# A decoder block on one core: x of the second half scaled sooner, the conv debt's floor lowered, two gate row buffers, and products of the identity in the opening

## The chip, the cores and the metric

One core of one Trainium2 chip runs the whole block. The metric is the device time of one execution in microseconds (us), lower is better. PE is TensorE (matmul), DVE is VectorE, ACT is ScalarE, POOL is GpSimd, SP is the queue engine that issues most transfers.

## The reference

The sequence has 2048 rows of 1024 channels, all in float32. Cut to what matters here:

```python
mod = silu(c) @ w_ada + b_ada
shift, scale, gate = split(mod, 3)
h = rms_norm(x, norm_w) * (1 + scale) + shift
a, b, g_conv, q, k, v, g_attn, m_conv, m_attn = split(h @ w_in)
u = depthwise_causal_conv(a * sigmoid(b), conv_w, conv_b)      # 31 taps
u = silu(layer_norm(u)) * silu(g_conv);  y_conv = u @ w_conv_out
q, k = rope(rms_norm(q), positions), rope(rms_norm(k), positions)
o = softmax-merge of 3 dilated window attentions (12 heads)
y_attn = (o * silu(g_attn)) @ w_attn_out
y = sigmoid(m_conv) * y_conv + sigmoid(m_attn) * y_attn
out = x + gate * (y @ w_out)
```

## The kernel before

All products keep float32 accuracy by splitting each operand into a high and a low part and adding three products (high by high, high by low, low by high). One block of 512 columns thus costs 12 matmuls, all issued from one line (L345); the kernel calls such a block a slot. Most of the projection is a Strassen-like scheme: a quad of blocks in seven products instead of eight, with sums of x and of the weights made by DVE and POOL.

The projection runs as 566 slots in four stages: q, k and v of the first half of the sequence (slots 0 to 131), its conv inputs and gates (132 to 285), then q, k, v (286 to 411) and conv and gates (412 to 565) of the second half. A planner written in Python walks over the slots. At each slot it prepares weights three slots ahead, runs what an agenda holds for that slot (`at_slot`), and spends a credit of VectorE time on two lists of spare work: the conv taps (`ce`, `cq`, `co`) and the "later" operations, which are the scaling and Strassen sums of the second half's x (tiles `xl`, `xs`, 32 operations). The credit grows by `PACE` of the stage (and by `AFTER` in quiet slots), falls by the cost of what was issued, and has a floor and a ceiling.

PE always executes in program order. The other engines do so in slots 0 to 137 and 286 to 417; in the two gate stretches between, a list scheduler with its own estimates chooses their order.

**The opening.** Before slot 0, x's first 512 columns are squared (ACT), summed on PE (`x_sum`, L1017), copied by DVE as a row (`xrow`, L1022), transposed back by PE (L1026), made an inverse root (`xst`, L1028 and POOL), and spread over the partitions by PE (`x_spread`, L1034); DVE then multiplies x by it (L1039). Meanwhile PE multiplies the conditioning vector by its matrix (`ada_mm`, L1045), ACT copies the row (L1050), PE transposes it (`pt_ada`, L1056) and DVE makes `mod` (L1059, L1061). Quarters A11, A12, A21 and A22 of h are split by ACT (`A_hi`) and DVE (`A_lo`) in `first_part` (A11 and A12 at L1077 to L1082, A21 and A22 at L1084 and L1085; A12 and A22 need the second group of `mod`). The same chain runs for t=1, the second 512 columns, during slots 0 to 3 (its scaling is L1041). Between these, DVE reduces the rotary angles in steps of two 1024-wide operations and more (`angle_steps`, L1109 to L1113), with a sine on ACT (L1111); ACT then reorders the tables (`table_turn`, L1121, L1123).

**Around slot 53.** DVE applies the rotary tables, makes low parts of weights and x sums (`slB`, `S_lo`), and prepares the inverse root of k (`rwk`, L210 as all helper-issued DVE work), which PE spreads into `rsk` at L737.

**The gate row.** From slot 444 on DVE adds 16 rows of w_ada, 128x512 each, into `gate_sum`, each through a tile `wg` that a transfer fills (`gate_load` L1587, `gate_add`). The tag `wg` has one buffer.

Of the kernel before, what the change touches and what calls it, by code (L numbers as in the profile page):

```python
# [40 lines left out]
FIRST_GATES, BETWEEN = (1, 1), ((1, 2, 1, 2, 1, 2, 1, 3), (1, 1, 2, 1, 1, 2, 1, 4))  # L41
PACE, AFTER, AGAIN = (2.87, 3.15, 2.62, 2.85), (0.75, 0.1), 12
PLAIN_QK, LATER_END = 4, 65
# [20 lines left out]
def tile_hybrid_block(  # L64
# [444 lines left out]
    def at_slot(s, f, where="vec"):  # L509
        agenda.setdefault((s, where), []).append(f)  # L510
# [620 lines left out]
    def angle_steps(count):  # L1131
        for _ in range(count):
            f = next(turning, None)
            if f:
                f()
# [142 lines left out]
    for name in ("B21", "B22"):  # L1278
        for j in range(2):
            weight(j, name)  # L1280

    angle_steps(7)
    pm = bank("t", "xm0")
# [5 lines left out]
    for k in range(2):  # L1289
        ada_mm(0, acc, k)  # L1290
    st = x_roots(0, pm, rows)
    angle_steps(2)
    for k in range(2, 4):
        ada_mm(0, acc, k)
    pr = x_spread(0, st, bank("u", "xr0"))
    for k in range(4, KC):
# [3 lines left out]
    for k in range(4):  # L1300
        x_scale(k, 0, pr)
    ada_mod(0, ada_row(0, acc), "t")
    for k in range(4):
        first_part("A11", k, 0)
# [51 lines left out]
    for k in range(4, KC):  # L1356
        at_slot(1, lambda k=k: x_scale(k, 0, pr), "act")
    for s, count in ((0, 2), (1, 2), (2, 6)):
        at_slot(s, lambda count=count: angle_steps(count))
# [123 lines left out]
    def run_later(s):  # L1483
        k, f = later_todo.pop(0)
        f()
        if k < 2 and later_todo[0][0] != k:
            at_slot(s + 3, lambda: later_load(k + 2), "store")
            later_from[k + 2] = s + 6

# [94 lines left out]
    def gate_load(i):  # L1584
        k, half = divmod(i, 2)
        wa = aside["wg", i] = aside["gp"].tile([P, 512], F32, tag="wg", name=f"wg{i}")
        nc.sync.dma_start(wa, w_ada[P * k : P * k + P, 2 * D + 512 * half : 2 * D + 512 * half + 512])  # L1587
# [10 lines left out]
    def gate_bias(i):  # L1598
        br = aside["gp"].tile([P, 512], F32, tag="wg", name=f"b_gate{i}")
        nc.sync.dma_start(br[:1, :], b_ada[None, 2 * D + 512 * i : 2 * D + 512 * i + 512])  # L1600
        dst = aside["g"][:1, 512 * i : 512 * i + 512]
        vec.tensor_add(dst, dst, br[:1, :])

    def gate_sum(i):
        sl = slice(512 * i, 512 * i + 512)
        pg = bank("o", f"pg{i}")
        nc.tensor.matmul(pg, ones, aside["g"][:, sl], start=True, stop=True)
        row = aside["gp"].tile([P, 512], F32, tag="wg", name=f"gate_out{i}")
        nc.scalar.activation(row[:1, :], pg[:1, :], AF.Copy, scale=0.125)
        nc.sync.dma_start(gate_d[:, sl], row[:1, :])  # L1610

    s = where_of[gates_start[1] + 6][6]
    at_slot(s, gate_open, "enter")
    for i in range(2 * KC + 1):
        if i:
            at_slot(s + 2 * i, lambda i=i: gate_add(i - 1))
        if i < 2 * KC:
            at_slot(s + 2 * i, lambda i=i: gate_load(i))
    for i in range(2):
# [9 lines left out]
    for s, (i, n) in enumerate(slots):  # L1629
# [15 lines left out]
        if n == 0:  # L1645
            kind, *job = jobs[i]
            running[i] = kind(*job, columns[i][0])
        next(running[i], None)
# [11 lines left out]
        stage = (i >= gates_start[0]) + (i >= half_jobs) + (i >= gates_start[1])  # L1660
        rest = AFTER[i >= half_jobs] if not waiting and s > busy_until[0] and stage % 2 else 0.0
        credit = min(max(credit, -2.0) + PACE[stage] + rest - spent[0], 2.0)
        spent[0] = 0.0
# [435 lines left out]
```

## Time and profile before

| | |
|---|---|
| time, median of 3 runs | 2354.8 us (2352.3 to 2357.51) |
| the profiled execution's own time | 2360.98 us |
| its span in the trace | 2358.4 us |
| mean granted TensorE clock | 0.993 of full |

The span is what the trace covers; 2.6 us of the execution's own time lie around it. The profiled execution was 6.2 us above the median of the runs shown. Times inside the trace are counted from the start of the span.

### The profile page before, as it was taken

What the parts mean: (1) busy time and instruction counts of PE and PEld (TensorE: products, weight loads), DVE (VectorE), ACT (ScalarE), POOL (GpSimd) and SP (SyncE); (2) the same over time, 40 slices, a digit from 0 to 9 for tenths busy, and PEclk for the clock granted to TensorE, in tenths of its full rate; (3) what the DMA queues carried; (4) which work ended last, traced back from release to release, by engine and by line L of the source; (5) the groups of instructions that cost most, each with busy time, mean ns of one, the idle gap of its engine ahead of it and who ended that gap; (6) DMA issues with size and microseconds to landing.
All of it is one profiled execution on the core that took longest, in us unless ns stands there. A gap on an engine that the chain in (4) does not pass through costs nothing.

```text
span 2358.4 us, 34462 instructions
## 1 busy us (share of the span) xinstructions
PE 2290.8 (97%) x11438; PEld 1868.6 (79%) x11438; DVE 1690.2 (72%) x2792; ACT 1120.8 (48%) x2291; POOL 1108.2 (47%) x866
## 2 busy tenths in 40 slices
PE   7999899999999999999999999999999999999999
PEld 4776688887878888787888887887888888888887
DVE  6668664566969789859746446799997957787544
ACT  5744455555644444654555545553444444332221
POOL 2345444545577789956433342445566630000221
PEclk9999999999999999999999999999999999999999
DMA  7567566665554455643666665655444579875553
GB/s 277 188 214 235 169 173 216 190 211 190 168 192 152 148 181 178 204 139 100 203 181 189 206 191 182 213 180 164 139 141 146 174 255 319 285 236 188 179 161 103
DMA packets 300942, 445.76 MB, mean 189 GB/s; under 512 B 28759, under 2 KB 132311, under 8 KB 300765
## 3 DMA queue, kind: packets, MB, share of 16 engines
q1 hardware_dynamic: 286648, 418.37, 55.8%
q10 hardware_dynamic: 14116, 25.20, 2.8%
q8 instruction: 90, 1.47, 0.3%
q14 instruction: 88, 0.71, 0.1%
HBM read 282.37 MB, written 161.09 MB: 188 GB/s over the span
## 4 chain that ended last, share of the span: by engine, by line
PE 50%; DVE 4%; DMA 2%; ACT 1%; issue 1%; POOL 0%; SPq 0%; ACTq 0%; DVEq 0%; POOLq 0%
PE yc L1710 8%; PE oa L1992 4%; PE ya L1710 4%; PE paab L345 3%; PE pak L345 3%; PE pav L345 3%; PE paq L345 2%; PE oc L1992 2%; PE pag_ma_d L345 2%; PE pcab L345 2%; PE pag_g_d L345 2%; PE po L945 2%; PE pcv L345 1%; DMA wg<-in_w_ada_dram 1%; PE pcq L345 1%; PE pck L345 1%
## 5 line engine op out<-in xcount | busy, mean ns | idle before, releaser
L282 POOL TENSOR_TENSOR slT<-wT,shT 128x512 fp32r<-128x512 f32 x172 | 232.8, 1354 | 283.9 <-ACT shT L281 270.6
L282 POOL TENSOR_TENSOR slB<-wB,shB 128x512 fp32r<-128x512 f32 x152 | 203.5, 1339 | 151.2 <-ACT shB L281 136.6
L281 ACT ACTIVATE shB<-wB 128x512 fp32r<-128x512 f32 x222 | 139.7, 630 | 167.5 <-issue 35.1
L282 POOL TENSOR_TENSOR slT<-wB,shT 128x512 fp32r<-128x512 f32 x98 | 131.8, 1350 | 148.1 <-ACT shT L281 120.6
L210 DVE SCALAR_TENSOR_TENSOR ce<-us,pair_taps,ce 128x512 f32<-128x512 f32 x240 | 180.9, 754 | 6.2
L210 DVE SCALAR_TENSOR_TENSOR ce<-ut,chan,ce 128x512 f32<-128x512 f32 x240 | 179.2, 747 | 0.5
L281 ACT ACTIVATE shT<-wT 128x512 fp32r<-128x512 f32 x176 | 110.4, 627 | 119.9 <-PE paab L345 21.2
L210 DVE SCALAR_TENSOR_TENSOR cq<-ut,chan,cq 128x512 f32<-128x512 f32 x208 | 155.2, 746 | 4.1 <-ACT cq L412 4.0
L210 DVE CUSTOM_DVE_ANT_0 sm<-ps,mask,rqq 128x256 f32<-128x256 f32 (+1 forms) x192 | 78.0, 443 | 93.0 <-PE ps L880 45.2
L276 POOL TENSOR_TENSOR wB<-wB,wB 128x512 f32<-128x512 f32 x80 | 111.2, 1391 | 47.2 <-DVE slB L210 44.1
L281 ACT ACTIVATE shT<-wB 128x512 fp32r<-128x512 f32 x120 | 75.2, 627 | 63.3 <-PE paab L345 30.7
L922 ACT ACTIVATE pT<-ptp 128x512 f32<-128x512 f32 (+2 forms) x84 | 44.8, 533 | 89.9 <-PE ptp L917 89.7
L139 POOL TENSOR_SCALAR stf<-stf 128x4 f32<-128x4 f32 x4 | 1.9, 473 | 179.9 <-DVE stf L1748 143.1
L945 PE MATMUL po<-v,pT 128*128 128x128 f32 x560 | 81.8, 277 | 3.0 <-ACT pT L922 2.8
L1920 ACT ACTIVATE yh<-yq 128x512 fp32r<-128x512 f32 x48 | 27.3, 623 | 120.4 <-POOL yq L1914 44.7
L945 PEld LDWEIGHTS po<-v,pT 128*128 128x128 f32 x560 | 75.1, 191 | 10.2 <-ACT pT L922 3.8
L210 DVE TENSOR_TENSOR slB<-wB,shB 128x512 fp32r<-128x512 f32 x70 | 54.9, 786 | 30.5 <-ACT shB L281 27.5
L902 ACT ACTIVATE sm<-sm,osb 128x256 f32<-128x256 f32 (+1 forms) x128 | 58.5, 463 | 4.2 <-DVE osb L210 4.2
L1911 POOL TENSOR_TENSOR ys<-yq 128x512 f32<-128x512 f32 x8 | 11.4, 1426 | 100.5 <-DMA yq<-y_d 88.8
L276 POOL TENSOR_TENSOR wT<-wB,wB 128x512 f32<-128x512 f32 x40 | 56.3, 1407 | 1.1
L917 PE MATMUL ptp<-ident,sm 128*128 128x128 f32 x332 | 52.3, 273 | 2.8 <-DVE stm L210 2.4
L622 POOL TENSOR_TENSOR slB_q<-wB_q,shB_q 128x512 fp32r<-128x512 f32 x16 | 29.5, 1846 | 54.3 <-ACT shB_q L621 49.7
(896 smaller groups left out, 7854.3 us busy)
## 6 DMA issues: line engine op xcount, KB each, us to landing
wB<-in_w_in_dram SPq DMA_DIRECT2D x262, 256.0 KB, 3.8
wT<-tT_d SPq DMA_DIRECT2D x136, 256.0 KB, 3.0
tT_d<-wB SPq DMA_DIRECT2D x102, 256.0 KB, 3.4
qk<-qk_d SPq DMA_DIRECT2D x96, 256.0 KB, 4.2
v_d<-vev SPq DMA_DIRECT2D x48, 256.0 KB, 3.4
qk_d<-spare_hi SPq DMA_DIRECT2D x48, 256.0 KB, 3.8
qk_d<-spare_lo SPq DMA_DIRECT2D x48, 256.0 KB, 4.1
v<-v_d SPq DMA_DIRECT2D x96, 128.0 KB, 3.9
```

Of the source, the lines that this page charges most:

```text
L210: return f(out, *args, **kw)
L276: nc.gpsimd.tensor_tensor(dst, x0, x1, op=ALU.subtract)
L281: nc.scalar.activation(h, q[name], AF.Copy)
L282: eng.tensor_tensor(l, q[name], h.bitcast(F32), op=ALU.subtract)
L345: nc.tensor.matmul(ps, x, y, start=(first and m == 0), stop=(last and m == 11), skip_group_check=True)
L622: nc.gpsimd.tensor_tensor(last[1], q[name], last[0].bitcast(F32), op=ALU.subtract)
L902: nc.scalar.activation(sm[:, a:z], sm[:, a:z], AF.Exp, scale=-1.0, bias=box["low"][i], accum_out=box["total"][i])
L917: nc.tensor.transpose(pt[:, c : c + P], box["sm"][:, c : c + P], ident)
L922: nc.scalar.activation(valid(pT), valid(pt), AF.Copy)
L945: nc.tensor.matmul(po[:, P * i : P * i + P], box["pT"][:, c : c + P], vt, start=(m == 0), stop=(m == count[i] - 1))
L1710: nc.tensor.matmul(pz, w, xx, start=(m == 0), stop=(m == len(terms) - 1))
L1992: nc.tensor.matmul(ps, y, w, start=(m == 0 and ps.name not in begun), stop=(m == 11 and not more), skip_group_check=True)
```

## The change

Idle products of a 128x128 identity by itself go into an unused bank, at five places of the opening: 10 at the start, 2 before the transpose L1026, 2 before `x_spread`, 4 before the row copy L1050 and 8 before the first slot. One angle step of two leaves slot 1 for later slots; x_scale of the first 512 columns' second half of channels moves from slot 1 to slot 2. Loads of the later x come one slot sooner after their trigger. `wg` gets two buffers, and each gate add stands three slots behind its load. The constants of the credit change: two entries of `PACE`, both of `AFTER`, the floor from -2 to -4, and 0.6 us a slot more in the four jobs of `qkv_plain` (slots 16 to 47).

```diff
-PACE, AFTER, AGAIN = (2.87, 3.15, 2.62, 2.85), (0.75, 0.1), 12
+PACE, AFTER, AGAIN = (2.87, 2.9, 2.62, 2.7), (1.0, 0.25), 12
...
+    idle_bank = bank("o", "idle")
+
+    def idle_products(count):
+        for _ in range(count):
+            nc.tensor.matmul(idle_bank[:, :P], ident, ident, start=True, stop=True)
+
+    idle_products(10)
     angle_steps(7)
...
         ada_mm(0, acc, k)
+    idle_products(2)
     st = x_roots(0, pm, rows)
     angle_steps(2)
     for k in range(2, 4):
         ada_mm(0, acc, k)
+    idle_products(2)
     pr = x_spread(0, st, bank("u", "xr0"))
...
         x_scale(k, 0, pr)
+    idle_products(4)
     ada_mod(0, ada_row(0, acc), "t")
+    idle_products(8)
     for k in range(4):
         first_part("A11", k, 0)
...
     for k in range(4, KC):
-        at_slot(1, lambda k=k: x_scale(k, 0, pr), "act")
-    for s, count in ((0, 2), (1, 2), (2, 6)):
+        at_slot(2, lambda k=k: x_scale(k, 0, pr), "act")
+    for s, count in ((0, 2), (1, 1), (2, 5), (3, 2)):
         at_slot(s, lambda count=count: angle_steps(count))
...
-            at_slot(s + 3, lambda: later_load(k + 2), "store")
-            later_from[k + 2] = s + 6
+            at_slot(s + 2, lambda: later_load(k + 2), "store")
+            later_from[k + 2] = s + 5
...
-        wa = aside["wg", i] = aside["gp"].tile([P, 512], F32, tag="wg", name=f"wg{i}")
+        wa = aside["wg", i] = aside["gp"].tile([P, 512], F32, tag="wg", name=f"wg{i}", bufs=2)
...
-    for i in range(2 * KC + 1):
-        if i:
-            at_slot(s + 2 * i, lambda i=i: gate_add(i - 1))
-        if i < 2 * KC:
-            at_slot(s + 2 * i, lambda i=i: gate_load(i))
+    for i in range(2 * KC):
+        at_slot(s + 2 * i, lambda i=i: gate_load(i), "load")
+        at_slot(s + 2 * i + 3, lambda i=i: gate_add(i))
...
-        rest = AFTER[i >= half_jobs] if not waiting and s > busy_until[0] and stage % 2 else 0.0
-        credit = min(max(credit, -2.0) + PACE[stage] + rest - spent[0], 2.0)
+        rest = AFTER[i >= half_jobs] if not waiting and s > busy_until[0] and stage % 2 else 0.6 * (jobs[i][0] is qkv_plain)
+        credit = min(max(credit, -4.0) + PACE[stage] + rest - spent[0], 2.0)
```

The first place is DVE in slots 0 to 2 of the opening, as a difference of before (-) and of the change (+). `spare_hi` holds the angles, `hf_0` is x of the first 512 columns, `xm` and `xrow` belong to the second 512.

```order
 L1109 SCALAR_TENSOR_TENSOR spare_hi<-spare_hi 128x1024
-L1039 TENSOR_TENSOR hf_0_176<-hf_0_176,xr_323 128x512 x2
-L1039 TENSOR_TENSOR hf_0_177<-hf_0_177,xr_323 128x512 x2
 L1109 SCALAR_TENSOR_TENSOR spare_hi<-spare_lo,spare_hi 128x1024
+L1022 COPY xrow_491<-xm_438 128x128
+L1028 TENSOR_SCALAR xst_494<-xm_438 128x4
+L1039 TENSOR_TENSOR hf_0_176<-hf_0_176,xr_338 128x512 x2
+L1039 TENSOR_TENSOR hf_0_177<-hf_0_177,xr_338 128x512 x2
 L1109 SCALAR_TENSOR_TENSOR spare_hi<-spare_hi 128x1024
```

Four multiplications and one angle operation that stood ahead of `xrow` stand behind it. Further on, L1112 and L1113 move from ahead of the scaling of `hf_1` (L1041) and the low parts of A21 (L1085) to behind them, just before `mod` of the second group (L1059).

The second place is DVE around slots 45 to 47. Before, the rows that end at a rotary operation on k (`tmk`):

```order
L210 SCALAR_TENSOR_TENSOR xl_1645<-xl_1645,mod,rsx 128x512
L210 TENSOR_TENSOR S_lo_1743<-s_1_1705,S_hi_1742 128x512
L210 TENSOR_TENSOR xs_2_1809<-xl_1639,xl_1643 128x512
L210 SCALAR_TENSOR_TENSOR xl_1643<-xl_1643,edge,xl_1645 128x512
L210 SCALAR_TENSOR_TENSOR xl_1639<-xl_1643,mod,xl_1639 128x512
L210 SCALAR_TENSOR_TENSOR tmk_1_00_1823<-spare_lo,hw,cos_988 128x512
```

The rows of the change that end at the same `tmk`:

```order
L210 SCALAR_TENSOR_TENSOR xl_1619<-xl_1619,mod,xl_1617 128x512
L210 SCALAR_TENSOR_TENSOR xl_1713<-xl_1713,mod,rsx 128x512
L210 SCALAR_TENSOR_TENSOR xl_1715<-xl_1715,mod,rsx 128x512
L210 TENSOR_TENSOR S_lo_1787<-s_1_1748,S_hi_1786 128x512
L210 SCALAR_TENSOR_TENSOR xl_1717<-xl_1717,mod,rsx 128x512
L210 SCALAR_TENSOR_TENSOR xl_1719<-xl_1719,mod,rsx 128x512
L210 TENSOR_TENSOR xs_3_1851<-xl_1713,xl_1717 128x512
L210 SCALAR_TENSOR_TENSOR tmk_1_00_1863<-spare_lo,hw,cos_1015 128x512
```

Of the 32 later operations six more stand ahead of this `tmk`, and so ahead of the second `rwk`, which follows 16 rows behind it in both. Behind that `rwk` nine are left before (three in slot 55, two in slot 56, four in slots 61 to 63) and three now (all in slot 56).

The third place is DVE in slots 452 to 454, ahead of the conv input `ut` of the third channel group. Before:

```order
L210 SCALAR_TENSOR_TENSOR gate_sum<-wg_16353,sc,gate_sum 128x512
L210 SCALAR_TENSOR_TENSOR ce_1_15844<-us_1_15962,pair_taps,ce_1_15844 128x512 x3
L210 TENSOR_TENSOR spare_lo<-spare_lo,pcab_2_15757 128x512
L210 SCALAR_TENSOR_TENSOR gate_sum<-wg_16402,sc,gate_sum 128x512
L210 SCALAR_TENSOR_TENSOR ce_1_15844<-us_1_15962,pair_taps,ce_1_15844 128x512
L210 SCALAR_TENSOR_TENSOR ut_2_15819<-spare_lo 128x2x256
L210 SCALAR_TENSOR_TENSOR ce_1_15844<-us_1_15962,pair_taps,ce_1_15844 128x512
L210 SCALAR_TENSOR_TENSOR ut_2_15819<-spare_lo,paab_2_15689 128x2x256
```

Of the change:

```order
L210 SCALAR_TENSOR_TENSOR gate_sum<-wg_16672,sc,gate_sum 128x512
L210 SCALAR_TENSOR_TENSOR ce_1_15891<-us_1_16012,pair_taps,ce_1_15891 128x512
L210 SCALAR_TENSOR_TENSOR gate_sum<-wg_16729,sc,gate_sum 128x512
L210 SCALAR_TENSOR_TENSOR ce_1_15891<-us_1_16012,pair_taps,ce_1_15891 128x512
L210 TENSOR_TENSOR spare_lo<-spare_lo,pcab_2_15780 128x512
L210 SCALAR_TENSOR_TENSOR gate_sum<-wg_16776,sc,gate_sum 128x512
L210 SCALAR_TENSOR_TENSOR ce_1_15891<-us_1_16012,pair_taps,ce_1_15891 128x512
L210 TENSOR_TENSOR gate_sum<-gate_sum,b_gate_16923 1x512
L210 SCALAR_TENSOR_TENSOR ut_2_15846<-spare_lo 128x2x256
L210 SCALAR_TENSOR_TENSOR ut_2_15846<-spare_lo,paab_2_15711 128x2x256
```

All 16 gate adds now stand ahead of this `ut`, where nine stood; the conv operations that they displace stand behind it, and the second `ut` operation keeps its place in DVE's order to within two operations (48 operations from the first gate add to it, 46 before). Besides these places and the idle products, the orders differ only by three conv operations, which move from slot 282 to slot 295 on DVE, and by the transfers and POOL and ACT rows that go with the moves told here.

## Rows read from the trace of the kernel before

**Rows 1.** The page, busy time of PE: us, share of the span, instructions.

```profile
PE 2290.8 (97%) x11438; PEld 1868.6 (79%) x11438; DVE 1690.2 (72%) x2792; ACT 1120.8 (48%) x2291; POOL 1108.2 (47%) x866
```

**Rows 2.** Opening by windows: length, each engine's busy us, granted clock, DMA.

```profile
26.30:29.70 3.40, 3.12 (x7) 2.51 (x8) 2.80 (x6) 3.37 (x6) 0.07 (x1) 0.50 1.05 405
...
39.90:43.30 3.40, 3.40 (x9) 2.62 (x8) 3.03 (x3) 0.27 (x1) 1.93 (x1) 0.50 0.03 11
```

**Rows 3.** Timeline of PE: start, duration, line, operation, [idle before, releaser].

```profile
22.74 0.44 PE L1056 MATMUL pt_ada<-ident,row 128*128 128x128 f32 x2 [1.89 <-ACT row L1050]
...
26.58 0.80 PE L345 MATMUL pC<-A_lo,shB_p 128*128 128x512 f32 x1 [0.81 <-DVE A_lo L1082]
...
34.99 1.30 PE L1017 MATMUL xm<-xsq,ones 128*32 128x128 f32 x40
39.28 0.33 PE L1026 MATMUL xm<-ident,xrow 128*128 128x128 f32 x1 [2.99 <-DVE xrow L1022]
...
43.80 1.05 PE L1034 MATMUL xr<-ident,xst 128*128 128x128 f32 x8
```

**Rows 4.** Timeline of DVE in the opening.

```profile
34.16 2.47 DVE L1039 TENSOR_TENSOR hf<-hf,xr 128x512 f32<-128x512 f32 x4
...
37.80 1.23 DVE L1109 SCALAR_TENSOR_TENSOR spare_hi<-spare_hi 128x1024 f32<-128x1024 f32 x1
38.95 0.28 DVE L1022 COPY xrow<-xm 128x128 f32<-128x128 f32 x1
...
45.22 1.23 DVE L1112 TENSOR_TENSOR spare_hi<-spare_hi 128x1024 f32<-128x1024 f32 x1 [2.22 <-ACT spare_hi L1111]
...
53.42 0.17 DVE L1059 TENSOR_TENSOR mod<-pt_ada,cols 128x8 f32<-128x8 f32 x1 [0.53 <-PE pt_ada L1056]
```

**Rows 5.** Timeline of ACT in the opening.

```profile
43.03 2.15 ACT L1111 ACTIVATE spare_hi<-spare_hi 128x1024 f32<-128x1024 f32 x2 [7.50 <-DVE spare_hi L1110]
...
53.32 2.03 ACT L1121 ACTIVATE ada_hi<-spare_hi 128x1024 f32<-128x1024 f32 x1
55.26 1.51 ACT L1077 ACTIVATE A_hi<-hf,mod 128x512 fp32r<-128x512 f32 x2
```

**Rows 6.** Groups on DVE, 145 to 210 us: count, busy us, mean ns, idle before.

```profile
L210 DVE SCALAR_TENSOR_TENSOR xl<-xl,mod,rsx 128x512 f32<-128x512 f32 x8 | 7.8, 1000 | 0.0
L210 DVE TENSOR_TENSOR S_lo<-s,S_hi 128x512 fp32r<-128x512 f32 x4 | 5.4, 1339 | 2.1 <-ACT S_hi L193 2.1
...
L210 DVE SCALAR_TENSOR_TENSOR xl<-xl,mod,xl 128x512 f32<-128x512 f32 x5 | 3.7, 749 | 0.6 <-DMA h_d<-xl 0.5
```

**Rows 7.** Waits of PE, 200 to 275 us: total us, times, longest.

```profile
PE rsk L737 <- DVE rwk L210: 5.8, 2, 3.2
PE pssk L688 <- ACT sqk L669: 2.2, 1, 2.2
...
PE pcv L345 <- DVE spare_hi L210: 1.1, 1, 1.1
```

**Rows 8.** Window around the first of the two waits for `rwk`.

```profile
207.20:214.00 6.80, 5.65 (x13) 4.04 (x14) 5.38 (x9) 1.12 (x2) 0.34 (x1) 0.50 0.90 234
```

**Rows 9.** Timeline of PE at the seam of the halves.

```profile
986.65 0.50 PE L345 MATMUL pav<-A_hi,shB 128*128 128x512 f32 x1 [2.98 <-ACT spare_hi L490]
```

**Rows 10.** Tile `wg`: its loads, who waited for it, time to landing.

```profile
L1587 SPq DMA_DIRECT2D wg<-in_w_ada_dram x16: 327/328/401, 1571.0 to 1638.9; - x16
...
  DMA wg<-in_w_ada_dram: 5.1, 7
...
DMA to landing us min/median/max: 2.6/2.9/3.6
```

**Rows 11.** Timeline of PE and of ACT around slot 456.

```profile
1614.36 0.79 PE L345 MATMUL pag_mc_d<-S_hi,shT 128*128 128x512 f32 x1 [4.60 <-ACT spare_hi L360]
...
1612.59 0.69 ACT L412 ACTIVATE cq<-ut,chan 128x512 f32<-128x512 f32 x1 [3.23 <-DVE ut L210]
```

**Rows 12.** Window behind that wait.

```profile
1613.50:1620.30 6.80, 5.94 (x14) 4.68 (x15) 6.34 (x10) 2.12 (x5) 2.60 (x3) 0.50 0.50 149
```

More of the change, by code (lines that the diff above doesn't have):

```diff
@@ L1598, in gate_bias @@
     def gate_bias(i):
-        br = aside["gp"].tile([P, 512], F32, tag="wg", name=f"b_gate{i}")
+        br = aside["gp"].tile([P, 512], F32, tag="wg", name=f"b_gate{i}", bufs=2)
         nc.sync.dma_start(br[:1, :], b_ada[None, 2 * D + 512 * i : 2 * D + 512 * i + 512])
@@ L1607, in gate_sum @@
         nc.tensor.matmul(pg, ones, aside["g"][:, sl], start=True, stop=True)
-        row = aside["gp"].tile([P, 512], F32, tag="wg", name=f"gate_out{i}")
+        row = aside["gp"].tile([P, 512], F32, tag="wg", name=f"gate_out{i}", bufs=2)
         nc.scalar.activation(row[:1, :], pg[:1, :], AF.Copy, scale=0.125)
@@ L1645, in tile_hybrid_block @@
         if n == 0:
-            kind, *job = jobs[i]
-            running[i] = kind(*job, columns[i][0])
+            running[i] = jobs[i][0](*jobs[i][1:], columns[i][0])
         next(running[i], None)
```

## The prediction

> **What bounds the kernel now.** I read the page's busy times first. PE is busy for 2290.8 us of a span of 2358.4 [rows 1], so all waits of PE together are 67.6 us, and no other engine is near the bound. A change that leaves the 566 slots alone can only win from these 67.6 us, from stretches at the lower clock, or lose by adding to either. I therefore looked for PE's waits at the places where the order moves, then for what the releaser had been doing, then for the granted clock behind the wait. Four places remain.
>
> In the opening PE waits 2.99 us at 39.28 for the row copy on DVE, which stands behind four multiplications and two angle operations [rows 3, 4], and behind the wait the clock is at half, 1.2 GHz, for 3.4 us [rows 2]. Around 208 us PE waits for `rwk` and pays again with 6.8 us at half clock [rows 7, 8]. At 986.65 it waits 2.98 for ACT at the seam of the halves [rows 9]. At 1614.36 it waits 4.60 for an ACT copy, which had stood behind another ACT operation that waited for DVE's `ut`; another 6.8 us at half clock follow [rows 11, 12]. A stretch at half clock costs about half its length where PE is busy in it: 1.7 us for 3.4, and about 3 us for 6.8 with 5.65 to 5.94 busy.
>
> **The idle products.** 26 products of 128 columns. The nearest row is `x_spread`: eight instructions for four float32 products of the same shape in 1.05 us, 0.26 a product [rows 3], or twice that at half clock. The last groups of 4 and 8, 1 and 2 us (2 and 4 at half clock), lie in PE's waits at 22.74 (1.89) and just behind it, where slot 0 waits for A11: its second product starts at 26.58 only when DVE's `A_lo` is there [rows 3]. The four low parts of A11 follow one another at DVE's pace, so slot 0's end is DVE's. I cost them at nothing; without this cover the 8 would cost 2 to 4 us. Their gain is also about nothing: the stretch of half clock from 26.3 [rows 2] lies in the same slot 0, where matmuls have only 3.12 us of work in 3.4 and wait for the low parts.
>
> The row shows the clock at 0.50 right behind waits of 1.89 and 0.81 us [rows 2, 3]. The Trainium skill ("TensorE: Matmul & The Clock Gate", Part 1: The HAM clock gate) says that the throttled clock is the default and that activity releases it. This trace agrees in the direction. By that rule the products keep the clock up and slot 0 runs at full speed; by the row the slot waits for DVE anyway.
>
> **The opening's order.** The row copy loses four multiplications (2.47 us) and one angle operation (1.23) ahead of it [rows 4]. It could start at 38.95 - 3.70 = 35.25, but the sums it copies end on PE at 34.99 + 1.30 = 36.29 [rows 3]. So it starts at about 36.4, 2.5 us sooner, and PE's wait of 2.99 shrinks to some 0.5. PE is then about 2.5 us ahead, 4.2 if the half-clock stretch behind it also goes. What does that meet? DVE does the same work in the same time: but it now waits for PE's sums from about 35.4 to 36.3, so the sine of 2.15 us starts 0.9 later than 43.03, at 43.9 [rows 5]. Before, DVE idled 2.22 us for the sine [rows 4]. Now it fills that time with the first two scalings of A21, but the first low part of A21 needs ACT's high part, which stands behind the sine: 43.9 + 2.15 + 0.75 (half of 1.51, a row of the same form [rows 5]) = 46.8. From there DVE has what it did between 45.22 and 53.42, less the 0.53 wait and less the two scalings (1.4 us, an estimate from 0.75 a scalar operation [rows 6] issued back to back): 46.8 + 8.2 - 0.5 - 1.4 = 53.1. The turn of the table on ACT (53.32) and A12's high part behind it (55.26) [rows 5] move by about 0.3. From there on ACT's rows follow one another without a pause through A12 and the tables up to A22. So of PE's 2.5 to 4.2 us about **0.3** remain; the rest becomes waits in slots 4 to 6. Bounds: a gain of 5.9 (4.2, and 1.7 of the first stretch) if ACT does not bind; a loss of 1.4 if the new wait brings a stretch at half clock (1.7 less 0.3).
>
> **Slots 36 to 65.** Six more later operations stand ahead of the second `rwk`. They last 0.75 where alone and 1.0 on average [rows 6]: 4.5 to 6.0 us busy, and some 4.4 in the pitch of 0.66 to 0.74 that back-to-back starts show. DVE's own idle time ahead of that `rwk` that they can fill is 2.1 + 0.5 = 2.6 us [rows 6]. So `rwk` is about 4.4 - 2.6 = 1.8 us later, and PE's wait of 3.2 there [rows 7] becomes 5.0. Behind it six operations are gone. Two of these leave slots 55 and 56, where DVE waited for PE anyway. The other four leave slots 61 to 63, where one to two operations stand between DVE's last wait for PE and PE's waits of 1.1 (`pcv`) and 2.6 (5.8 - 3.2, the next `rwk`) [rows 7]: 0.75 to 1.9 back, I take 1.1. The wait for `sqk` (2.2) [rows 7], with one operation more ahead of it in slot 56, I raise by 0.3. Sum 1.8 + 0.3 - 1.1 = **+1.0**. Bounds: -3 (the six operations wholly in DVE's idle time, the relief full, one stretch of half clock shorter), +6 (below). Queued behind these operations on SP are the loads of `xl`, moved one to three slots up, which go past the loads of `s` and weights; no wait of PE's in rows 7 names a transfer, so I cost that at nothing, up to +2.
>
> **Seam.** Three conv operations (0.75 each) leave slot 282, ahead of the ACT operation that PE waits 2.98 for. I take **-0.4**, between nothing and -2.2.
>
> **The gate row.** 16 loads are issued over 67.9 us, and DVE waited for them 5.1 us in seven waits [rows 10]. With one buffer a load starts only when the add before it is done. With two, two adds share a landing time of 2.9 plus an add of 0.75 and some 0.4 of issue: about 4.1 us, one add per 2.05. All 16 adds now stand ahead of `ut`, within 48 DVE operations instead of 46. At a mean pitch of 0.75 these are 36 us, 15 intervals of 2.05 are 30.8: the adds are supplied on average, but the last eight stand every second or third row, 1.5 to 2.2 us apart, so some of them wait 0.5. Before `ut` I put 2 us of waits in place of about 3.4; plus two operations, 1.5. So `ut` comes at the same time to 0.1 us, the wait of 4.60 and its half-clock stretch [rows 11, 12] stay. Behind `ut` DVE has seven adds less and waits no more: **-0.8**, a short wait of PE of 0.6 at 1642 and a little more. Bounds: +4 (landing 3.6 each time: 2.4 an add, 36 us of supply against the last eight in 15 us), -8.
>
> The Trainium skill ("DMA: Bandwidth & Descriptors", Anatomy of one DMA) puts a fixed part of about 2 us into each transfer, whatever its size, which a second buffer overlaps. The landing of 2.9 us for 256 KB agrees. By its formula (an estimate from that page, 2.0 + 0.6 = 2.6) the cadence would be 1.9 instead of 2.05, and the sum the same.
>
> **The constants of the credit** move no operation beyond those counted: in both gate stretches the scheduler's order is as before. They cost nothing.
>
> Sum: -0.3 + 1.0 - 0.4 - 0.8 = -0.5 on an execution of 2360.98, which stood 6.2 above the median. On the median of 2354.8 that is 2354.3.
>
> **The rivals.**
> Small net effect, as above (chance 0.45): 2354.3, from 2349 to 2359.
> The gate row pays (0.20): the waits for `wg` vanish, `ut` comes 2 to 3 us sooner, PE's wait falls to 2 and the half-clock stretch goes: 2.6 + 3.0 + 0.6 = 6.2 us, with the other terms (-0.3 + 1.0 - 0.4) 2348.9. For it: 5.1 us of waits on an engine without pause there. Against it: the copy waits in ACT's order for the whole of DVE's queue, which grew by two operations.
> The opening pays (0.14): the clock stays up and ACT is not the end of the chain: -5.9, with the other terms (-0.2) 2348.7. For it: two stretches at half clock [rows 2]. Against it: ACT's unbroken work from A12 on. It is the way by which the rule on the clock would decide. With the gate row as well (0.05): 2342.
> Slower (0.16): `rwk` at 208 us. If the six operations cost their busy 6.0 us and none of the idle time absorbs them, because `S_lo` still waits for ACT, PE's wait becomes 9.2 and the clock stays low longer: +6, with the relief of 1.1, the other terms of -1.5 and 3 more for a longer half clock: 2354.8 + 6.4 = 2361. It decides once `rwk` is over 4 us later.
>
> **How the numbers follow.** 0.2% (4.7 us) is about what a measurement can tell from no change. Faster by more: the gate row, the opening and both (0.39, of which 0.05 fall just inside), and 0.06 from the small case's edge: 0.40. Slower: 0.16 plus 0.01. Same: 0.43. The range reaches from 2345 (it leaves out the double gain) to 2360.5.
>
> **What would show it.** In the changed trace: the wait for `xrow` under 1 us and new waits of PE before A12 at 53 to 58 us; ACT's turn of the table at 53; the wait for the second `rwk` at 4.5 to 5.5; seven or fewer waits for `wg` of 2 to 3 us in sum; the wait near 1614 still above 3. I am wrong if that last wait is gone, if slot 10 starts more than 2 us sooner, or if the second `rwk` wait exceeds 7.

## Result and profile after

The changed kernel takes 2364.77 us (median of 7 runs, 2362.16 to 2370.33) against 2356.53 for the kernel before in its 7 runs: a ratio of 1.0039, 95% interval 1.0025 to 1.0054, so 5.9 to 12.7 us slower. The forecast was 2354.3, with 0.17 for slower. The rival "slower: `rwk` at 208 us" is the nearest to what happened; the place is right for the larger of the two losses, the reason is not. Its own point, 2361, lay above the stated range, which ended at 2360.5.

The page of the changed kernel, busy time of each engine; the order of the lines is that of [rows 1]:

```profile
span 2365.3 us, 34571 instructions
...
PE 2303.2 (97%) x11490; PEld 1876.2 (79%) x11490; DVE 1693.8 (72%) x2792; ACT 1121.3 (47%) x2291; POOL 1104.3 (47%) x866
```

PE is busier by 12.4 us and its waits are 62.1 us in place of 67.6. That is not a faster kernel: PE's busy time holds the idle products and the matmuls that run at half clock. Sums over the whole span don't show where the time went; a ruler along the program does better. The start of a slot is the start of its first matmul of L345, and every slot has 12. The start in the changed kernel less that in the kernel before, in us, with each stretch's own share:

```
slot      0     2     4     6    16    46    72   136   446   466   565
less  -0.11 -2.62 -3.89 +0.49 +2.34 +2.34 +6.87 +6.90 +7.64 +6.56 +6.52
here        -2.51 -1.27 +4.38 +1.85  0.00 +4.53 +0.03 +0.74 -1.08 -0.04
```

By this one pair of traces two places lose and one gains. The opening first wins 3.9 us by slot 4, then loses 6.2 by slot 16. Slots 46 to 72 lose 4.5. The gate row wins 1.1.

How much of that is chance can be read from the experiments below: a run that leaves a stretch of slots alone is one more profile of the kernel before there. The length of the stretch less that in the kernel before, in us:

| slots | runs that leave the stretch alone | changed kernel |
|---|---|---|
| 0 to 16 | -0.04 to +0.05 (six: e5 to e8, e11, e12) | +2.45 |
| 46 to 72 | -5.81 to +1.43 (six: e1 to e3, e7 to e9) | +4.53 |
| 136 to 446 | -5.41 to +7.69 (ten: all but e4 and e10) | +0.74 |
| 446 to 466 | -3.48 to -1.18 (seven: e1 to e3, e5, e6, e8, e9) | -1.08 |

So the loss of the opening is far from chance. That of slots 46 to 72 lies outside it, but its size is uncertain by some us on the ruler. Slots 136 to 446 say nothing, and the gain of the gate row is none: the kernel before was slower there in its one profile than in any of the seven runs with the same code.

**Opening.** Windows of the changed kernel (columns as in [rows 2]); the first two are the stretches that stood at half clock before.

```profile
26.30:29.70 3.40, 2.90 (x9) 1.46 (x9) 2.79 (x6) 3.37 (x6) 0.17 (x1) 1.00 1.05 405
39.90:43.30 3.40, 3.40 (x19) 2.93 (x20) 3.33 (x3) 0.00 (x0) 0.00 (x0) 1.00 0.03 10
60.40:63.80 3.40, 3.40 (x9) 2.28 (x9) 3.09 (x6) 3.37 (x4) 1.29 (x1) 0.50 0.36 128
```

Both stretches are at full clock now, and a new one at 1.2 GHz stands at 60.4. Timelines of the changed kernel, PE, then DVE, then ACT, answering to [rows 3 to 5]:

```profile
26.47 0.50 PE L345 MATMUL pC<-A_lo,shB_p 128*128 128x512 f32 x1 [0.82 <-DVE A_lo L1082]
...
36.66 0.33 PE L1026 MATMUL xm<-ident,xrow 128*128 128x128 f32 x1 [0.48 <-DVE xrow L1022]
...
51.19 0.44 PE L1056 MATMUL pt_ada<-ident,row 128*128 128x128 f32 x2 [1.47 <-ACT row L1050]
...
57.85 0.49 PE L345 MATMUL pC<-A_hi,shB_p 128*128 128x512 f32 x1 [2.09 <-ACT A_hi L1077]
```

```profile
36.31 0.29 DVE L1022 COPY xrow<-xm 128x128 f32<-128x128 f32 x1 [0.93 <-PE xm L1017]
...
46.85 0.75 DVE L1085 SCALAR_TENSOR_TENSOR A_lo<-hf,mod,A_hi 128x512 fp32r<-128x512 f32 x1 [1.51 <-ACT A_hi L1084]
...
51.05 2.30 DVE L1112 TENSOR_TENSOR spare_hi<-spare_hi 128x1024 f32<-128x1024 f32 x1
53.38 1.66 DVE L1113 TENSOR_SCALAR spare_hi<-spare_hi 128x1024 f32<-128x1024 f32 x1
54.96 0.15 DVE L1059 TENSOR_TENSOR mod<-pt_ada,cols 128x8 f32<-128x8 f32 x1
```

```profile
44.06 2.15 ACT L1111 ACTIVATE spare_hi<-spare_hi 128x1024 f32<-128x1024 f32 x2 [8.63 <-DVE spare_hi L1110]
...
55.08 2.02 ACT L1121 ACTIVATE ada_hi<-spare_hi 128x1024 f32<-128x1024 f32 x1 [3.43 <-DVE spare_hi L1113]
57.00 1.51 ACT L1077 ACTIVATE A_hi<-hf,mod 128x512 fp32r<-128x512 f32 x2
```

The reader is to see that the chain went as worked out up to 51.05 (the row copy at 36.31, the sine at 44.06, A21's first low part at 46.85), and then L1112 takes 2.30 us where it took 1.23 [rows 4], and L1113 1.66 where it took 0.69 (first line below, of the kernel before). POOL works beside them in the changed kernel (second line); the same two POOL operations took 2.59 us before, when DVE did other work (third line):

```profile
46.48 0.69 DVE L1113 TENSOR_SCALAR spare_hi<-spare_hi 128x1024 f32<-128x1024 f32 x1
```

```profile
50.94 3.55 POOL L327 TENSOR_TENSOR slB_p<-wB_p,shB_p 128x512 fp32r<-128x512 f32 x2 [12.58 <-ACT shB_p L326]
```

```profile
52.70 2.59 POOL L327 TENSOR_TENSOR slB_p<-wB_p,shB_p 128x512 fp32r<-128x512 f32 x2 [10.82 <-ACT shB_p L326]
```

ACT's turn of the table (L1121) waits 3.43 us for L1113 and starts at 55.08 in place of 53.32, and A12's high part, which stands behind it on ACT, starts at 57.00 in place of 55.26.

**Slots 46 to 72.** Waits of PE in the changed kernel over the same slots as [rows 7]:

```profile
PE rsk L737 <- DVE rwk L210: 8.8, 2, 5.8
PE pssk L688 <- ACT sqk L669: 2.9, 1, 2.9
...
PE pcq L345 <- DVE slT L210: 1.1, 1, 1.1
PE pcv L345 <- DVE spare_hi L210: 0.4, 1, 0.4
```

The wait for the second `rwk` is 5.8 instead of 3.2. PE's waits from slot 46 to 72 come to 16.2 us instead of 12.5 (10.7 to 12.6 in the six runs that leave this stretch alone), with the same 13.7 us at half clock. On DVE the second `rwk` starts 31.1 us after slot 46 on PE instead of 27.2 (26.8 to 27.4 in those six runs); this measure hardly depends on the clock, which was at half for 3.4 to 17.1 us of this stretch in those runs. What DVE did ahead of it, in the changed kernel's timeline:

```profile
169.59 0.74 DVE L210 SCALAR_TENSOR_TENSOR xl<-xl,mod,xl 128x512 f32<-128x512 f32 x1
174.63 0.75 DVE L210 SCALAR_TENSOR_TENSOR xl<-xl,mod,xl 128x512 f32<-128x512 f32 x1 [4.30 <-DMA h_d<-xl]
```

SP's timeline of the same time (columns alike), then the wait of SP's queue in it, and last SP's timeline in the kernel before:

```profile
165.68 4.79 SPq L1453 DMA_DIRECT2D xl<-in_xt_dram  x4
170.57 0.85 SPq L1456 DMA_DIRECT2D h_d<-xl  x2
```

```profile
SPq L1453 <- DMA s_d<-xl: 1.8, 1, 1.8
```

```profile
164.28 0.64 SPq L1445 DMA_DIRECT2D h_d<-xl  x1
165.20 2.00 SPq L1442 DMA_DIRECT2D xl<-in_xt_dram  x4
167.24 0.43 SPq L1445 DMA_DIRECT2D h_d<-xl  x1
```

DVE overwrites an `xl` tile in place, and must wait until the store of its old value to `h_d` has read it. That store stands on SP behind four loads of the third `xl` set. The loads take SP from 165.68 to 170.47, 1.8 us of it in a wait for a buffer that an `s_d` store still reads. In the kernel before the four loads took 2.00 us and only one of the stores stood behind them. DVE's one wait for an `h_d` store there was 0.5 us, later, at 189.73 [rows 6].

**Gate row.** Tile `wg` in the changed kernel, as [rows 10], and then PE's wait around slot 456, from its waits:

```profile
L1598 SPq DMA_DIRECT2D wg<-in_w_ada_dram x16: 327/328/423, 1578.7 to 1614.1; - x16
...
  DMA wg<-in_w_ada_dram: 3.8, 6
```

```profile
PE pag_mc_d L345 <- ACT spare_hi L360: 5.0, 1, 5.0
```

16 loads in 35.4 us instead of 67.9, 3.8 us of waits instead of 5.1, and the wait of PE stays: 5.0 against the 4.6 of [rows 11].

### The profile page after: what moved, and what is told of

The parts are those of the page before. It is cut to its first block, busy times and chain, and to the rows that moved or that the text cites. A ratio compares the mean times of both kernels' runs of the same rounds, so it can differ in the third digit from the quotient of the medians.

```text
span 2365.3 us, 34571 instructions
## 1 busy us (share of the span) xinstructions
PE 2303.2 (97%) x11490; PEld 1876.2 (79%) x11490; DVE 1693.8 (72%) x2792; ACT 1121.3 (47%) x2291; POOL 1104.3 (47%) x866
## 3 DMA queue, kind: packets, MB, share of 16 engines
q8 instruction: 90, 1.47, 0.3%
## 4 chain that ended last, share of the span: by engine, by line
PE 51%; DVE 3%; DMA 1%; ACT 1%; issue 1%; POOL 1%; SPq 0%; ACTq 0%; DVEq 0%; POOLq 0%
PE yc L1718 8%; PE oa L2000 4%; PE ya L1718 4%; PE paab L345 3%; PE pak L345 3%; PE paq L345 2%; PE pav L345 2%; PE oc L2000 2%; PE pag_ma_d L345 2%; PE pcab L345 2%; PE pag_g_d L345 2%; PE po L945 2%; PE pcq L345 1%; PE pck L345 1%; PE pcv L345 1%; PE pag_mc_d L345 1%
## 5 line engine op out<-in xcount | busy, mean ns | idle before, releaser
L276 POOL TENSOR_TENSOR wB<-wB,wT 128x512 f32<-128x512 f32 x40 | 54.9, 1372 | 0.0
```

Source lines behind the costliest of these rows:

```text
L276: nc.gpsimd.tensor_tensor(dst, x0, x1, op=ALU.subtract)
```

## The experiments

Each ratio is to the kernel before, measured beside it. The intervals are 0.1 to 0.15% to each side, too wide for single parts of 1 or 2 us; the slot ruler in each run's trace is therefore read first and the time second. The ruler has chance in it too, behind the waits from slot 46 on (table above and last section). Up to slot 46, where only the opening's part acts, it repeats: slot 16 is within 0.26 us of the kernel before in all six experiments that leave the opening's order alone (e5 to e8, e11 and e12). Each edit is shown as a cut, against the kernel before unless another is named.

**e1_opening_alone.**

```diff
+    idle_products(10)
...
-        at_slot(1, lambda k=k: x_scale(k, 0, pr), "act")
-    for s, count in ((0, 2), (1, 2), (2, 6)):
+        at_slot(2, lambda k=k: x_scale(k, 0, pr), "act")
+    for s, count in ((0, 2), (1, 1), (2, 5), (3, 2)):
```

> The kernel before with the opening's part of the change alone (idle products, angle steps, x_scale). Theory A: two POOL operations at 51 to 54 us run beside L1112 and L1113 in their new place and stretch them from 1.9 to about 4 us, mod of the second group, the table's turn and A12's high part come 1.7 us late, PE waits 2 us and runs 3.4 us at half clock. Then slot 16 starts 2.3 us (2.0 to 2.6) later than before, the time is 2.3 us more, and from slot 46 to 72 nothing is added. Rival B: the opening's loss in the changed kernel came from somewhere else (loads, clock phase): slot 16 within 0.7 us of before.

Slot 16 is 1.91 us late, just under theory A's range, slot 72 2.00; L1112 took 2.31 and L1113 1.65, and A12's high part starts at 57.13. Ratio 1.0012 (1.0001 to 1.0023). The loss of the opening belongs to its own part, and slots 46 to 72 add nothing without the others. The two operations stand beside POOL here as well; whether that is the whole cause needs the next run. The stretch at half clock lies at 52.2 here, not at 60.4.

**e2_roots_early.** Against e1_opening_alone:

```diff
-    for s, count in ((0, 2), (1, 1), (2, 5), (3, 2)):
+    for s, count in ((0, 2), (1, 1), (2, 7)):
```

> As e1_opening_alone, with L1112 and L1113 put back ahead of the low parts of A21, where POOL is idle. Theory A (overlap with POOL): they take 1.9 us together again, A12's high part starts at about 54.5 instead of 57.0, the stretch at half clock near 60 us goes, slot 16 starts 0.8 us (0.2 to 1.4) sooner than before. Rival B (the sine 0.9 us later is the cause, wherever the two stand): A12's high part at 56 to 57, slot 16 1.5 to 2.5 us later than before.

```profile
46.26 1.23 DVE L1112 TENSOR_TENSOR spare_hi<-spare_hi 128x1024 f32<-128x1024 f32 x1 [2.21 <-ACT spare_hi L1111]
47.52 0.69 DVE L1113 TENSOR_SCALAR spare_hi<-spare_hi 128x1024 f32<-128x1024 f32 x1
...
54.72 0.17 DVE L1059 TENSOR_TENSOR mod<-pt_ada,cols 128x8 f32<-128x8 f32 x1 [0.78 <-PE pt_ada L1056]
```

In this kernel's DVE timeline the two operations are back at 1.23 and 0.69 away from POOL, as theory A had it. But A12's high part starts at 56.34 (A: 54.5, B: 56 to 57), and slot 16 is 2.08 late. So A alone falls, and both of rival B's numbers came: with the overlap gone A12's high part is still 1.08 later than before, since the sine is at 44.08, 1.05 later than before; putting the two operations behind A21's low parts and beside POOL adds another 0.79 (57.13 in e1). This split holds for A12. At slot 16 it can't be read: slot 16 is a whole us later than A12 says, in a trace with the clock at half from 52.3 for 6.8 us, twice as long as in e1. Ratio 0.9997 (0.9985 to 1.0009).

**e3_roots_late.** Here L600's copies overwrite the angles before the turns read them, so the rotary tables aren't the reference's; the operations and their shapes are the same. Against e1_opening_alone:

```diff
-    for s, count in ((0, 2), (1, 1), (2, 5), (3, 2)):
+    for s, count in ((0, 2), (1, 1), (2, 5), (5, 2)):
-    ... enumerate(((1, 4, 5), (2, 5, 6), (1, 6, 7), (2, 6, 7))):
+    ... enumerate(((1, 8, 9), (2, 8, 9), (1, 9, 10), (2, 9, 10))):
...
-        at_slot(4, lambda i=i: table_keep(0, i), "store")
+        at_slot(8, lambda i=i: table_keep(0, i), "store")
```

> As e1_opening_alone, with L1112 and L1113 behind the low parts of A12 and the four turns of the table on ACT moved from slots 4 to 6 to slots 8 and 9. Theory A: mod of the second group waits for neither, A12's high part starts at about 52, PE keeps most of the 3.9 us that it is ahead at slot 4, slot 16 starts 3 us (2 to 4) sooner than before. Rival C (ACT's chain to A22 is full whatever stands in it, as the prediction had it): slot 16 within 0.7 us of before.

A12's high part starts at 52.32, as expected, and A22's at 62.62 instead of 69.26 in e1: ACT's chain is not full without the turns, so rival C is wrong in its reason. Yet slot 16 is only 0.85 sooner than before, not 3. PE's gain went into slots 4 and 5: the wait of 1.47 for the copy of the conditioning row on ACT (L1050), half clock from 51.9 for 3.4 us, and short waits for DVE's low parts of A21. In their third place L1112 and L1113 stand beside POOL again (its two operations start at 57.55) and take 2.33 and 1.67 again. Ratio 0.9998 (0.9988 to 1.0009).

**e9_scale_behind_row.**

```diff
+    idle_products(10)
...
-        at_slot(1, lambda k=k: x_scale(k, 0, pr), "act")
+        at_slot(2, lambda k=k: x_scale(k, 0, pr), "act")
```

> The kernel before with the idle products, and of the opening's order only the four multiplications moved behind the row copy; both angle operations stay ahead of it, L1112 and L1113 stay ahead of A21's low parts. Theory A2 (the loss is the sine, late because DVE waits 0.93 us for PE's sums ahead of the row copy, and L1112 beside POOL): the row copy starts at about 36.6 with no wait of DVE, the sine at 43.1 instead of 44.1, A12's high part at 55.3 as before, slot 16 within 0.4 us of before (1.7 more if the new waits of PE bring a stretch at half clock). Rival E (any PE that runs ahead in slots 2 to 4 loses it at half clock behind the wait): slot 16 1.5 us or more later than before even with A12's high part at 55.3.

```profile
43.16 2.15 ACT L1111 ACTIVATE spare_hi<-spare_hi 128x1024 f32<-128x1024 f32 x2 [7.61 <-DVE spare_hi L1110]
...
55.43 1.50 ACT L1077 ACTIVATE A_hi<-hf,mod 128x512 fp32r<-128x512 f32 x2
```

The sine is back at 43.16, A12's high part at 55.43, and slot 16 at 0.33: theory A2 stands, although a stretch at half clock (53.4, 3.4 us) lies behind PE's new waits. PE had been 2.35 us ahead at slot 4 and lost all of it. Ratio 0.9989 (0.9976 to 1.0002). So the loss of the opening comes from the order of the angle operations: one less ahead of the row copy, which leaves DVE 0.93 us idle on the way to the sine, and L1112 and L1113 in a place beside POOL.

**e8_idle_alone.**

```diff
+    idle_products(10)
...
+    idle_products(8)
```

> The kernel before with the 26 idle products alone, in its own order of the opening. By the prediction's step: the stretch at half clock at 26.3 goes, but slot 2 starts within 0.3 us of before since DVE's low parts and the row copy set it; slot 16 within 0.5 us of before unless the stretch at 39.9 goes too (then 1.7 less). Rival: the higher clock shows, slot 2 or slot 16 starts 1.5 us or more sooner.

The window from 24 to 31 us, first of the kernel before, then of this one:

```profile
24.00:31.00 7.00, 4.92 (x20) 3.41 (x20) 5.48 (x8) 6.53 (x10) 1.73 (x3) 0.76 1.05 401
```

```profile
24.00:31.00 7.00, 5.46 (x29) 2.90 (x28) 5.48 (x8) 6.51 (x10) 1.72 (x3) 1.00 1.05 402
```

The clock is full and DVE's and ACT's work the same: slot 2 starts at +0.01, slot 16 at -0.03. The products do keep the clock up: all five runs without them (the kernel before, e5, e6, e7, e11) have a stretch at half clock that begins between 24.0 and 26.3 us, and none of the eight other runs with them has one there. But nothing comes of it. The stretch at 39.9 was gone too, for which the expectation gave 1.7 us: slot 4 did start 1.57 sooner, a wait of 1.47 for ACT's row copy (L1050) took it back, and slot 6 starts at -0.01. The ratio is 0.9985 (0.9971 to 0.9999), which the slots to 16 don't explain and e12_gate_loads_idle doesn't repeat.

**e4_stores_first.** The changed kernel, with SP's order alone altered.

```diff
-            at_slot(s + 2, lambda: later_load(k + 2), "store")
+            at_slot(s + 3, lambda: later_load(k + 2), "load")
```

> The changed kernel, only SP's order differs: the loads of the third and fourth xl stand behind the three stores and the load of s that they went ahead of; the order on all other engines is the same. Theory S: DVE's wait of 4.30 us for the store h_d at 174 us is the loss in slots 46 to 72; it falls under 0.7 us, the lateness that PE gathers from slot 46 to 72 (4.5 us) falls to 0.7 (0 to 1.5), the time falls by about 3.8. Rival D: the six operations themselves, stretched beside POOL, are the loss: 4 us or more of the 4.5 stay, the time within 1 us of the changed kernel.

From slot 46 to 72 PE loses 1.16 us instead of 4.53, its wait for the second `rwk` is 2.3 instead of 5.8, and that `rwk` starts 28.9 us after slot 46 instead of 31.1. The wait for `h_d` at 174 is gone; another, 2.29 us, appears at 186.53, behind the next set of loads, which theory S didn't have. Ratio 1.0020 (1.0009 to 1.0031), against 1.0039: theory S, by the ruler and by the time.

**e5_loads_sooner_alone** and **e6_credit_alone** take the two edits of that region one by one from the kernel before.

```diff
-            at_slot(s + 3, lambda: later_load(k + 2), "store")
-            later_from[k + 2] = s + 6
+            at_slot(s + 2, lambda: later_load(k + 2), "store")
+            later_from[k + 2] = s + 5
```

> The kernel before with the loads of the third and fourth xl one slot sooner and nothing else; two h_d stores then stand behind four xl loads on SP, DVE's order is as before to within two operations. Theory S (the store behind the loads is the loss): DVE waits 1 to 4 us for an h_d store near 172 us instead of 0.5, and PE is 1 to 3 us later at slot 72 than before. Rival D (the number of operations ahead of the second rwk): nothing changes, slot 72 within 0.5 us.

```diff
-        rest = AFTER[...] if not waiting and s > busy_until[0] and stage % 2 else 0.0
+        rest = AFTER[...] if not waiting and s > busy_until[0] and stage % 2 else 0.6 * (jobs[i][0] is qkv_plain)
```

> The kernel before with 0.6 us a slot more of credit in slots 16 to 47 and nothing else; four to six more operations stand ahead of the second rwk, and the h_d stores stay ahead of the xl loads on SP. Theory S: DVE waits under 1.5 us for h_d, PE is at most 1.5 us later at slot 72 than before. Rival D: PE's wait for the second rwk grows from 3.2 to 5 us or more and slot 72 is 2 to 4.5 us later.

Neither does harm. With the loads alone DVE waits 0.49 us for `h_d` at 172, which misses what theory S gave (1 to 4), though two stores do stand behind the loads and SP is held by `s_d` stores here as well (e5's timelines of SP and DVE, then SP's wait):

```profile
165.25 1.96 SPq L1442 DMA_DIRECT2D xl<-in_xt_dram  x4
167.26 0.90 SPq L1445 DMA_DIRECT2D h_d<-xl  x2
```

```profile
172.19 0.75 DVE L210 SCALAR_TENSOR_TENSOR xl<-xl,mod,xl 128x512 f32<-128x512 f32 x1 [0.49 <-DMA h_d<-xl]
```

```profile
SPq L1442 <- DMA s_d<-xl: 7.1, 4, 5.5
```

What differs is when DVE asks. Counted back from the start of slot 46, the two stores leave 13.0 us ahead of it in e5 and 12.2 in the changed kernel; DVE comes to the tile 8.6 us ahead in e5 and, with the credit that brings the later operations forward, 12.4 in the changed kernel. With the credit alone DVE doesn't wait for `h_d` at all: four more later operations stand ahead of the second `rwk`, which starts 27.4 us after slot 46 (27.2 before), and PE waits 1.7 for it; slot 72 starts at -0.72 (-0.26 at slot 46). Ratios 0.9986 (0.9974 to 0.9998) and 1.0001 (0.9988 to 1.0014). Rival D falls for four operations: they filled DVE's idle time. Six without any wait for a store were not run.

**e10_changed_loads_back.** The changed kernel with the distance of the loads as before.

```diff
-            at_slot(s + 2, lambda: later_load(k + 2), "store")
-            later_from[k + 2] = s + 5
+            at_slot(s + 3, lambda: later_load(k + 2), "store")
+            later_from[k + 2] = s + 6
```

> The changed kernel with the loads of the third and fourth xl back at their old distance; the two h_d stores stand ahead of them again, one operation less stands ahead of the second rwk. Theory S: DVE waits under 1.5 us for h_d, from slot 46 to 72 PE loses 1.0 us (0 to 2) instead of 4.5, the opening's 2.0 us at slot 16 stay, the time is 3.5 us below the changed kernel and about 0.15% above the kernel before. Rival D: 4 us or more of the 4.5 stay.

DVE has the order of the changed kernel up to 12.4 us ahead of slot 46, where that one waited 4.30, and goes on without a wait; its only wait for `h_d`, later, is 0.31 us. The second `rwk` starts 27.7 us after slot 46; from slot 46 (+1.84) to slot 72 (+1.16) PE even gains 0.7. Its SP timeline has the stores first, and the loads take nearly as long without holding them:

```profile
163.77 2.56 SPq L1456 DMA_DIRECT2D h_d<-xl  x3
...
166.98 3.91 SPq L1453 DMA_DIRECT2D xl<-in_xt_dram  x4
```

Ratio 1.0017 (1.0006 to 1.0028), median 2360.33: 4.4 us below the changed kernel's (the kernel before stood at 2357.78 beside the one and 2356.53 beside the other). So it takes both edits: with the shorter distance the loads stand ahead of two stores and are held by a buffer that isn't free yet, and with the credit DVE wants the stored tile before the stores have left. The pair without the rest of the change was not run.

**e7_gate_alone.**

```diff
-        wa = ... tag="wg", name=f"wg{i}")
+        wa = ... tag="wg", name=f"wg{i}", bufs=2)
...
-            at_slot(s + 2 * i, lambda i=i: gate_add(i - 1))
-            at_slot(s + 2 * i, lambda i=i: gate_load(i))
+        at_slot(s + 2 * i, lambda i=i: gate_load(i), "load")
+        at_slot(s + 2 * i + 3, lambda i=i: gate_add(i))
```

> The kernel before with the gate row's part alone (two buffers, adds three slots behind their loads). By the prediction's step: DVE's waits for wg are 3 to 4 us in sum (5.1 before), PE's wait near 1614 stays between 3 and 6, from slot 446 to 466 PE gains 1.1 us (0.5 to 2.0); time 1 us less, not to be told from no change. Rival: the wait near 1614 halves and the time falls by 4 us or more.

Waits for `wg` 3.0 us in five, PE's wait near 1614 is 4.2, and from slot 446 to 466 PE gains 2.5 us by this trace (1.1 in the changed kernel). Ratio 0.9993 (0.9982 to 1.0005), 1.6 us less at the middle and not told from none.

That gain is the profile of the kernel before, not the edit: the seven other runs that leave the gate row alone are 1.2 to 3.5 us shorter than it there, the six with the edit 1.1 to 2.5. In those seven PE's wait near 1614 is 2.3 to 3.4 us and the second operation of `ut` starts 27.2 to 28.2 us after slot 446; with the edit the wait is 4.2 to 5.0 and `ut` comes at 29.0 to 30.0. The profile before, with 4.6 and 29.5, is the odd one of its kind. The edit does take 0.6 us of PE's waits away at 1642, but it brings `ut` 1 to 2 us later, not sooner.

**e11_gate_and_loads** and **e12_gate_loads_idle** put together what had done no harm: e5's and e7's edits, and in the second the idle products as well.

> The kernel before with the gate row's part and the sooner loads of xl, without credit, opening order and idle products. If the two single gains (0.07% and 0.14%) are real and add: 0.9979, about 5 us less than before. If they are chance: within 0.1% of before; by slots, 1.1 us less from the gate row and nothing else.

> As e11_gate_and_loads, with the 26 idle products in the order of before. If the single gain of the idle products (0.15%) is real: 0.9964, about 8 us less than before, 3.5 less than e11_gate_and_loads. If slot 16 tells it rightly (no change): the same as e11_gate_and_loads to 0.1%.

Ratios 0.9987 (0.9976 to 0.9999) and 0.9998 (0.9984 to 1.0012), medians 2353.93 and 2355.59 against 2357.78. The single gains don't add up to what either sum asked for (0.9979 and 0.9964), and the idle products add nothing that can be told. e11's interval just excludes no change, as e5's and e8's do; with twelve versions compared, none can be called a clear gain.

## Why the prediction was wrong

**Opening: -0.3 forecast, +2.3 measured.** The steps up to DVE's arrival at L1112 were right to 0.1 us each (sine 43.9, measured 44.06; first low part 46.8, 46.85), and so was the reading that ACT's and DVE's chain, not PE, sets A12. The step that failed is the price of what followed: "From there DVE has what it did between 45.22 and 53.42" carried over 1.9 us for L1112 and L1113 from a place where POOL is idle to one where POOL works; they took 3.9. Without these 2.0 us A12's high part would have started at about 55.0 (an estimate: 57.00 less 2.0), where the forecast had it at about 55.6; it started 1.74 later than before. Slot 16 is late by another 0.6, in a trace with half clock at 60.4, which had stood as a bound and was valued at nothing. e9 shows the other way out: with both angle operations ahead of the row copy the sine isn't late, L1112 and L1113 can stay where POOL is idle, and slot 16 is at +0.33.

The Trainium skill (SBUF — State Buffer, SBUF: two separate sides) says that VectorE and GpSimd share a port pair under an exclusive lock, held for a whole instruction. The rows agree: L1112 reads two SBUF operands and takes 2.30 beside POOL and 1.23 away from it, L1113 1.66 and 0.69, each about one us more, and POOL's two operations 3.55 instead of 2.59. The prediction did not ask what POOL does at 51 us. The kernel before had the price in its own trace: beside the same kind of POOL operations two L1109 take 2.34 and 2.20 us, where L1109 takes 1.23 at 37.80 [rows 4].

```profile
29.62 3.54 POOL L327 TENSOR_TENSOR slB_p<-wB_p,shB_p 128x512 fp32r<-128x512 f32 x2 [5.27 <-ACT shB_p L326]
```

```profile
29.67 2.34 DVE L1109 SCALAR_TENSOR_TENSOR spare_hi<-spare_lo,spare_hi 128x1024 f32<-128x1024 f32 x1
32.04 2.20 DVE L1109 SCALAR_TENSOR_TENSOR spare_hi<-spare_hi 128x1024 f32<-128x1024 f32 x1
```

**Slots 36 to 65: +1.0 forecast, +5.0 measured (+4.5 over slots 46 to 72).** The step that failed is "no wait of PE's in rows 7 names a transfer, so I cost that at nothing, up to +2". PE never waits for these transfers; DVE does, and PE waits for DVE. The 4.30 us for `h_d` took the place of the 2.6 us of DVE's idle time that were to absorb the six operations: DVE's idle time between the first and second `rwk` rose from 2.58 to 4.30 us. So the second `rwk` came 3.9 us later, not 1.8. The operations themselves were priced too high, not too low: with four of the six ahead of that `rwk` and no wait for the store at 174 (e6, e10) it comes 0.2 to 0.5 us later. The ruler over slots 46 to 72 (-0.5 and -0.7 there) is within chance and can't give their price. The rival for "slower" had the place, and "over 4 us later" is near the 3.9, but the wrong mechanism, "`S_lo` still waits for ACT": in the changed kernel it does not wait at all.

**Seam: -0.4 forecast, 0.0.** PE's wait there is 3.0 as before. **Gate row: -0.8 forecast, -1.1 on the ruler, and that is luck.** The waits for `wg` did fall and the wait near 1614 did stay, but the gain comes from one slow profile of the kernel before (e7). Against the other runs the step "`ut` comes at the same time to 0.1 us" fails: it comes 1 to 2 us later. The formula that the prediction took from the Trainium skill (DMA: Bandwidth & Descriptors, Anatomy of one DMA) is given there for transfers that GpSimd issues. These loads go over SP's queue; in the changed kernel they landed in 2.7 to 4.9 us. **Idle products: nothing forecast, nothing measured**, for the reason given. The rule of the Trainium skill (TensorE: Matmul & The Clock Gate, Part 1: The HAM clock gate), that activity releases the throttled clock, agrees with the clock in these windows (0.76 and 1.00). **Credit:** beyond slots 36 to 65, where its part was counted, a trace of it could not be told from chance.

One sum is off as well: with the opening and the gate row both paying, the terms give 2354.8 - 5.9 - 6.2 + 0.6 = 2343.3, not 2342. And none of the three signs of being wrong came: the wait near 1614 is 5.0, slot 10 starts 2.52 us later and not sooner, the wait for the second `rwk` is 5.8. They watched the waits that the sum already had.

The terms on the ruler sum to +2.3 + 4.5 + 0.0 - 1.1 = +5.7, another 0.7 lies in slots 136 to 446, and the spans differ by 6.9. The medians differ by 8.2 and the two profiled executions by 6.2, so the ruler misses about 2 us of the usual difference. Where these lie isn't settled; the gate row, with its too slow profile before, may hold some.

## What to carry to other kernels

A transfer that must wait for a buffer holds what is queued behind it (here SP stood 1.8 us with two stores behind the loads). Before moving a load forward, look at which stores stand behind it and who waits to overwrite their source, also on an engine that is not the bottleneck: here that engine's 2.6 us of idle time were all the cover that the bottleneck had. Two edits that are harmless alone can meet in one queue, so the order of that queue is to be read for both together.

An operation's duration belongs to its place. When one is moved on VectorE, look at what GpSimd does in the new place before taking over the old number (1.23 us became 2.30 here); and follow a gain on the bottleneck to the next wait before booking it.

One profile of the kernel before is one draw. Runs that leave a place alone are more draws of it: they confirmed the two losses here and took away the gain of the gate row.

## What the runs showed of the hardware

The same wait goes with half clock for 3.4 us, for 6.8 us, or with none, in executions of nearly the same program. PE's wait of 3.18 us for `rwk` in slot 53 goes with 6.8 us at 1.2 GHz in the kernel before and in e1_opening_alone, and with 3.4 in e7_gate_alone, where it is as long. A half-clock stretch at PE's other wait for `rwk`, at 265 us and 6.8 us long in the kernel before, is missing in e7_gate_alone, whose wait there is as long: from slot 68 to 72 it gains 2.8 us for nothing that the change did. The spans of single profiles reach from 2345.1 us (e12_gate_loads_idle, 17.0 us at half clock ahead of its end) to 2364.6 (e8_idle_alone, 34.0 us), while the medians of both lie within 2 us of each other. At half the length of a stretch, the price that the prediction read from its rows, the clock explains some 8.5 of these 19.5 us (an estimate); the rest was not traced. A profile's span therefore says little about an edit of a few us. The ruler says more where runs that leave the stretch alone agree on it, and so do many executions.
